# One visit less per unit, a later start for unit 4's norms, two later solves and a folded gate step in a two-layer decoder step

## The chip, the cores and the metric

The kernel runs on one core of one Trainium2 chip. The metric is device time in microseconds (us) of one execution; shown are single executions and the median of three. Its engines are TensorE (PE, with its weight loads as PEld), VectorE (DVE), ScalarE (ACT), GpSimd (POOL) and SyncE (SP, which here only issues DMAs).

## The reference, cut to what matters

One inference step of two layers for one prompt (16 meta tokens + 256) and eight samples, so 280 columns in all, width 4096, 64 heads of 64. Layer A is RWKV-7 time mixing, layer B sliding-window attention on a key/value shared by both groups. The change lies in layer A:

```python
rkvz = einsum('btpd,pde->btpe', xm[:, :, :4], w_rkvz)          # four products of 2048 x 4096
a = sigmoid(a0 + (xa @ a1) @ a2)
kk = k_h * k_k;  kk = kk / maximum(sqrt(sum(kk*kk)), 1e-12)    # norms per head
k_h = k_h * (1 + (a_h - 1) * k_a)
b_h = kk * a_h
def rwkv7_step(S, inp):                                        # scanned over the 272 prompt tokens
    r, d, k, v, kk, b = inp
    sa = einsum('bhij,bhj->bhi', S, kk)
    S = S*d - sa*b + v*k
    return S, einsum('bhij,bhj->bhi', S, r)
y = groupnorm(y) + sum(r*k*r_k) * v
hp = hp + (y * silu(z)) @ w_out
```

## The kernel before, in words

Every large product is done in split single precision: weights and inputs are cut into a high and a low part (`split`: ACT casts the high part at L195, DVE subtracts at L197), and `mm3` (L218, L219, L220) adds three matmuls, high by high, high by low, low by high.

Layer A runs from about 140 to 1245 us. `drive` writes TensorE's order by hand. Its backbone is `products()`: 64 products (r, k, v, z by groups of heads, and half of the output product) of 16 *pieces* each, a piece being six matmuls of 128x280 into one of two banks; at a product's end its banks are evacuated by ACT (L790; in the output product by DVE, L785). Between pieces other streams put in small groups of fp32 matmuls or transposes, called *visits* here: a stream says `yield n` to let n pieces pass. All other engines get their order from a scheduler, in which an instruction written after a `yield` comes later, and each runs its list strictly in that order. SP's list holds the weight loads (`raw_...`, L211, one per two pieces) and all other transfers.

The 64 heads are worked on in 16 *units* u, two to each *round* o:

- `prep(u)` loads `rT`, spreads the norms of kk over partitions (`spread`, L563, a DMA `kk<-kr`; `kr` comes by L558 from a small matrix of norms that covers four units), forms `kk` (L898), the scan `cl` (L910), `kT` (L904) and the gate `ta` (the code's `a`): ACT's affine step L905 makes a -0.5 (tanh + 1) of it, L906 multiplies by `kk`. Later it copies six tiles to `sm` on POOL (L932), forms `rk` (L945) and its split, has `ps_sm` (L935) and `ps_bo` (L954) on TensorE. `prep_e(u)` fills `KB` from `kT`, `ta` and `cl` (L972, L973).
- `scores(u)` makes five visits: two for the whole chunks' scores (L1017 ...), one for the short chunk of 16 tokens (`ps_sc4`, eight matmul records at L1031) and one each for the transposes of the keys' blocks j = 0 and 1 (`ps_bk`, ten at L1049), whose results ACT copies to `BK`.
- After the scores of an odd unit `substitute` inverts 16x16 blocks on DVE (the tile `NL`, L1075 to L1077, ends in the stream transposes TN L1081 and TR L1082, read by ACT's L1085 as `TT`), and `solve(o)` needs `TN` for its first visit (`ps_so`, L1102), then DVE's and ACT's copies for three more (L1108, L1120, L1129).
- `chain(o)` (L1191 to L1227) carries the state through the chunks, `group_norm(o)` sends y back by transposes `ps_yt` (L1275, into `vT` on DVE, L1276), and `load_x`, `decode` (the samples), `late_gates` (the output product's inputs) run beside.

`scores` and `solve` of the odd units and `chain` are one stream (`main`): a `yield` added in it moves everything behind it by as many pieces, until it next waits for another stream.

Of the kernel before, what the change touches and what calls it, by code (L numbers as in the profile page):

```python
# [25 lines left out]
L = NM + SEQ  # L26
# [83 lines left out]
class Kernel:  # L110
# [747 lines left out]
    def prep(self, u):  # L858
        nc, rp, I = self.nc, self.rp, self.I
        V, A, G = nc.vector, nc.scalar, nc.gpsimd  # L860
        tt = V.tensor_tensor
        MU, AD, SU = ALU.mult, ALU.add, ALU.subtract
        dma = nc.sync.dma_start
        p0 = 2 * u
        b, sl = p0 // 4, slice(p0 % 4, p0 % 4 + 2)
        w = lambda n, bufs=1: rp.tile([128, 2, N], F32, tag=n, bufs=bufs, name=f"{n}{u}")

        raw = rp.tile([LR, 512], F32, tag="lraw", name=f"lraw_{u}")
        dma(raw, I['lw2'][u])
        if u:  # L870
            yield 3
        hi = rp.tile([128, 544], F32R, tag="lhi", name=f"lhi_{u}")[:LR, :512]
        lo = rp.tile([128, 544], F32R, tag="llo", name=f"llo_{u}")[:LR, :512]
        self.split(hi, lo, raw)
        ws = [(hi[:, 256 * i:256 * i + 256], lo[:, 256 * i:256 * i + 256]) for i in range(2)]
        wa = [w("cl"), w("ta")]
        for i, (hi, lo) in enumerate(ws):
            for j in range(2):
                yield 3 if i or j else 4 if u else 14, self.pp_free
                ps = self.pp_bank(f"ps_l{i}{j}_{u}")  # L880
                self.mm3(ps[:, :N], hi[:, j * 128:j * 128 + 128], lo[:, j * 128:j * 128 + 128],
                         self.lt[i][0], self.lt[i][1], True, True)
# [10 lines left out]
        dma(rT, self.rd[b][:, sl])

        kk = w("kk")
        self.spread(kk, self.kr[u // 4][4 * u % 16:4 * u % 16 + 4])
        for j in range(2):
            V.scalar_tensor_tensor(kk[:, j], kT[:, j], self.pcol(P_KK, p0 + j), kk[:, j], op0=MU, op1=MU)  # L898

        for j in range(2):  # L900
            km = rp.tile([128, N], F32, tag="sq", bufs=2, name=f"km{j}_{u}")
            A.activation(km, a[:, j], AF.Identity, scale=self.par2[:, 64 + p0 + j:65 + p0 + j],
                         bias=self.par2[:, 96 + p0 + j:97 + p0 + j])
            tt(kT[:, j], kT[:, j], km, op=MU)  # L904
        A.activation(a, a, AF.Identity, scale=-0.5, bias=self.half[:, 1:2])  # L905
        tt(a, a, kk, op=MU)  # L906
        A.activation(cl, cl, AF.Identity, scale=0.5, bias=self.half[:, 0:1])

        for j in range(2):
            V.tensor_tensor_scan(cl[:, j, :L], self.reset, cl[:, j, :L], 0.0, op0=MU, op1=AD)  # L910

        Pp = self.Pp
        ch = lambda x: x[:, :, :256].rearrange("p q (c t) -> p q c t", t=64)
        pch = Pp[:, :, :260].rearrange("p q (c t) -> p q c t", t=65)
        for j in range(2):
            A.activation(pch[:, j, :, 1:65], ch(cl)[:, j], AF.Exp, scale=-CD)
        A.activation(Pp[:, :, 261:N + 5], cl[:, :, 256:N], AF.Exp, scale=-CD)
# [12 lines left out]
        sm = rp.tile([128, 2, 6, NS], F32, tag="sm", name=f"sm{u}")  # L930
        for i, x in enumerate((kk, a, kT, rT, vT, Pp[:, :, 5:])):
            G.tensor_copy(sm[:, :, i], x[:, :, L:N])  # L932
        yield 8, self.pp_free
        ps = self.pp_bank(f"ps_sm{u}")
        nc.tensor.transpose(ps[:96, :128], sm.rearrange("p a b c -> p (a b c)"), self.ident)  # L935
        sr = rp.tile([96, 2, 64], F32, tag="sr", name=f"sr{u}")
        A.copy(sr, ps[:96, :128].rearrange("p (h j) -> p h j", h=2))  # L937
        g, h0 = p0 // 8, (2 * p0) % 16
        for j in range(2):
            dma(self.vecd[g][:, :, h0 + 2 * j:h0 + 2 * j + 2].rearrange("v b h j -> (v b) (h j)"),  # L940
                sr[48 * j:48 * j + 48].rearrange("p h j -> p (h j)"))

        def rk_of(j):
            rk = rp.tile([128, L], F32, tag="sq", bufs=2, name=f"rk{j}_{u}")
            V.scalar_tensor_tensor(rk, rT[:, j, :L], self.pcol(P_RK, p0 + j), kT[:, j, :L], op0=MU, op1=MU)  # L945
            self.split(two[0][:, j], two[1][:, j], rk)
        two = [rp.tile([128, 2, L], F32R, tag=n, name=f"rk{n}{u}") for n in ("lhi", "llo")]
        for j in range(2):
            rk_of(j)
        for j in range(2):  # L950
            yield 5 - j if u > 1 else 3, self.pp_free
            ps = self.pp_bank(f"ps_bo{j}_{u}")
            for i in range(2):
                nc.tensor.matmul(ps[:, :L], self.ones, two[i][:, j], start=i == 0, stop=i == 1)  # L954
            tt(vT[:, j, :L], ps[:, :L], vT[:, j, :L], op=MU)
            A.activation(vT[:, j, :L], vT[:, j, :L], AF.Identity, bias=self.pcol(P_GB, p0 + j))
        self.U[u] = dict(PC=self.PC, bonus=vT, kT=kT, rT=rT, kk=kk, a=a, cl=cl)

    def prep_e(self, u):
# [12 lines left out]
        tt(KB[:, :, 0:4, 0:64], ch(a), ch(cl), op=MU)  # L972
        tt(KB[:, :, 4, 0:16], a[:, :, 256:272], cl[:, :, 256:272], op=MU)  # L973
        A.copy(KB[64:128, :, :, 128:192], KB[64:128, :, :, 0:64])

        E = rp.tile([128, 5, 2, L], F32, tag="E", bufs=3, name=f"E_{u}")
# [7 lines left out]
    def scores(self, u):  # L984
        nc, rp = self.nc, self.rp

        odd = u % 2
        gap = iter((8, 3, 4, 3, 3) if odd else (8, 6, 6, 5, 4))
        turn = iter((0, odd, 0, odd, 0))
        def banks(nm):  # L990
            if next(turn):
                two = self.two_banks(f"ps_{nm[0]}{nm[1]}")
# [14 lines left out]
        for c0 in (0, 2):  # L1007
# [11 lines left out]
            for q in range(2):  # L1019
                pv, kr = ps[q], H(1 - q)  # L1020
                out = lambda i, r: E[r, i, :, 64 * c0:64 * c0 + 128].rearrange("p a (c t) -> p a c t", c=2)
                for r, a, t0 in ((64 * q, self.F, 0), (64 * q + 32, self.ND, 32)):
                    A.copy(inst(a, slice(r ^ 64 * odd, (r ^ 64 * odd) + 32), cs), pv[r:r + 32, :, :, t0:64])
                tt(out(q, kr), pv[kr, :, :, 0:64], bc(self.cst(C_MASK, 64, kr), 64, 2, 2, 64), op=MU)
                tt(out(3 + q, slice(0, 128)), pv[:, :, :, 64:128], bc(self.cst(C_MASK + 64, 64), 128, 2, 2, 64), op=MU)
        yield next(gap)
        ps = [b[:, :64].rearrange("p (a h t) -> p a h t", a=2, h=2) for b in banks(("sc", f"4_{u}"))]
        with self.pe_order():
            for j in range(2):
                for q in (1, 0):  # L1030
# [12 lines left out]
        for j in range(2):
            yield next(gap)
            ps = [b[:, :320].rearrange("p (c t) -> p c t", c=5) for b in banks(("bk", f"{j}_{u}"))]
            with self.pe_order():
                for c in range(5):
                    for q in (1, 0):
                        nc.tensor.transpose(ps[q][:, c], KB[H(q), j, c, 64 * q:64 * q + 128], self.ident[H(q), H(q)])  # L1049
            for q in range(2):  # L1050
                A.copy(BK[:, j, :, H(q)], ps[q])
# [37 lines left out]
    def solve(self, o):  # L1089
# [4 lines left out]
        ev = lambda n, *s: rp.tile([128, 512], F32, tag="ev", bufs=2, name=f"{n}{o}")[:, :s[0] * s[1]].rearrange(  # L1094
            "p (i t) -> p i t", t=s[1])

        yield 24 if o < 5 else 27
        ps = self.bank(self.pe, f"ps_so{o}")
        Q = [slice(32 * q, 32 * q + 32) for q in range(4)]
        for i in range(16):  # L1100
# [872 lines left out]
```

## Time and profile before

| | us |
|---|---|
| three runs | 2115.4, 2117.19, 2122.31 (median 2117.19) |
| profiled execution, whole | 2118.32 |
| its span | 2116.5 |
| TensorE busy in the span | 2064.9 (98%) |
| VectorE busy | 1697.8 (80%) |
| ScalarE busy | 1263.8 (60%) |
| GpSimd busy | 122.5 (6%) |
| mean granted TensorE clock | 0.99 of full speed |

The 1.8 us between the span and the whole execution lie outside the profile. TensorE's idle time, 51.6 us, is spread over the program, and an engine that is busy in the records may still be slow: the column PEclk of the profile's stretches gives the clock that it was granted. In the rows below a line is "start, duration, engine, line, operation, output<-input", and a bracket at the end holds how long the engine had stood idle before it and what released it.

### The profile page before, as it was taken

Reading aid. Unit: us, or ns where it says so; the run is one execution under the profiler, and the core shown is the slowest. Engines: PE = TensorE matmul, PEld = TensorE weight load, DVE = VectorE, ACT = ScalarE, POOL = GpSimd, SP = SyncE. Lnnn points to the kernel's source line nnn. Section 1 sums busy time; section 2 is a strip of 40 time slices with the busy share of each in tenths; the row PEclk is TensorE's granted clock in tenths of the full one; section 3 lists DMA queues with packets and bytes.
Section 4 is the critical chain, followed back from the end, with each engine's and each line's share of the span. In section 5 each row is a group of like instructions: output and inputs, shape, how many; then the busy total and the mean of one; then the engine's idle time right before and its main releaser. Section 6 shows DMA issues by size and latency. Waiting matters only on the chain.

```text
span 2116.5 us, 55871 instructions
## 1 busy us (share of the span) xinstructions
PE 2064.9 (98%) x21420; PEld 1965.8 (93%) x21420; DVE 1697.8 (80%) x4112; ACT 1263.8 (60%) x2790; POOL 122.5 (6%) x188
## 2 busy tenths in 40 slices
PE   9999999899999999999999999999999999999997
PEld 7999899889899989899999999999999999999997
DVE  8867777687678878888888788997888888878885
ACT  3457766576766757767676445565565655544443
POOL 0011100001010010100100001100000000000000
PEclk9999999999999999999999999999999999999999
DMA  7898667658756876777657687757455444567774
GB/s 258 314 312 250 189 213 241 188 181 290 216 180 205 260 229 198 211 217 222 203 152 246 207 257 243 247 172 227 132 167 156 146 155 130 181 210 247 232 219 132
DMA packets 276356, 446.28 MB, mean 211 GB/s; under 512 B 54056, under 2 KB 97768, under 8 KB 275696
## 3 DMA queue, kind: packets, MB, share of 16 engines
q1 hardware_dynamic: 275656, 441.66, 66.6%
q8 instruction: 168, 2.75, 0.5%
q10 hardware_dynamic: 432, 1.05, 0.1%
q14 instruction: 100, 0.82, 0.1%
HBM read 381.69 MB, written 65.03 MB: 211 GB/s over the span
## 4 chain that ended last, share of the span: by engine, by line
PE 87%; DVE 5%; ACT 3%; DMA 3%; issue 2%; SPq 0%; POOL 0%; DVEq 0%; POOLq 0%; ACTq 0%
PE ps_z L218 6%; PE ps_z L219 6%; PE ps_z L220 6%; PE ps_k L218 3%; PE ps_ob L218 3%; PE ps_ob L220 3%; PE ps_v L218 3%; PE ps_ob L219 3%; PE ps_r L218 3%; PE ps_q L218 3%; PE ps_q L220 3%; PE ps_q L219 3%; PE ps_k L219 3%; PE ps_k L220 3%; PE ps_v L220 3%; PE ps_v L219 3%
## 5 line engine op out<-in xcount | busy, mean ns | idle before, releaser
L218 PE MATMUL ps_z<-mhlm,whi_z 128*128 128x280 f32 x512 | 158.6, 310 | 2.8 <-ACT sr L937 2.0
L219 PE MATMUL ps_z<-mhlm,whi_z 128*128 128x280 f32 x512 | 150.6, 294 | 0.0
L220 PE MATMUL ps_z<-mhlm,wlo_z 128*128 128x280 f32 x512 | 150.3, 294 | 0.0
L218 PE MATMUL ps_q<-bmh,whi_qb 128*128 128x264 f32 x512 | 150.0, 293 | 0.1
L218 PE MATMUL ps_z<-bmh,whi_zb 128*128 128x264 f32 x512 | 147.4, 288 | 0.0
L220 PE MATMUL ps_q<-bmh,wlo_qb 128*128 128x264 f32 x512 | 145.6, 284 | 0.6 <-DVE wlo_qb L197 0.6
L219 PE MATMUL ps_q<-bml,whi_qb 128*128 128x264 f32 x512 | 145.6, 284 | 0.0
L219 PE MATMUL ps_z<-bml,whi_zb 128*128 128x264 f32 x512 | 145.5, 284 | 0.0
L220 PE MATMUL ps_z<-bmh,wlo_zb 128*128 128x264 f32 x512 | 145.4, 284 | 0.0
L218 PE MATMUL ps_ob<-ghi,whi_ob 128*128 128x264 f32 x512 | 145.3, 285 | 0.0
L220 PE MATMUL ps_ob<-ghi,wlo_ob 128*128 128x264 f32 x512 | 144.6, 284 | 0.0
L219 PE MATMUL ps_ob<-glo,whi_ob 128*128 128x264 f32 x512 | 144.6, 283 | 0.0
L195 ACT CAST whi_ob<-raw_ob 128x512 fp32r<-128x512 f32 x128 | 79.1, 620 | 96.9 <-PE ps_ob L219 77.8
L195 ACT CAST whi_oa<-raw_oa 128x512 fp32r<-128x512 f32 x128 | 79.2, 620 | 88.0 <-PE ps_oa L219 30.6
L197 DVE TENSOR_TENSOR wlo_r<-raw_r,whi_r 128x512 fp32r<-128x512 f32 x128 | 87.8, 691 | 42.6 <-ACT whi_r L195 41.3
L218 PE MATMUL ps_v<-mhlm,whi_v 128*128 128x280 f32 x384 | 119.8, 312 | 0.4 <-ACT st L790 0.4
L218 PE MATMUL ps_k<-mhlm,whi_k 128*128 128x280 f32 x384 | 119.1, 310 | 1.0 <-ACT st L790 1.0
L195 ACT CAST whi_v<-raw_v 128x512 fp32r<-128x512 f32 x128 | 79.0, 619 | 65.8 <-PE ps_v L219 37.7
L197 DVE TENSOR_TENSOR wlo_v<-raw_v,whi_v 128x512 fp32r<-128x512 f32 x128 | 87.3, 687 | 36.9 <-ACT whi_v L195 35.6
L195 ACT CAST whi_zb<-raw_zb 128x512 fp32r<-128x512 f32 x128 | 78.2, 619 | 62.9 <-PE ps_z L219 38.5
L220 PE MATMUL ps_k<-mhlm,wlo_k 128*128 128x280 f32 x384 | 112.4, 293 | 2.1 <-issue 2.1
L219 PE MATMUL ps_v<-mhlm,whi_v 128*128 128x280 f32 x384 | 112.7, 293 | 0.0
(478 smaller groups left out, 7604.1 us busy)
## 6 DMA issues: line engine op xcount, KB each, us to landing
raw_k<-a_w_rkvz SPq DMA_DIRECT2D x128, 256.0 KB
raw_v<-a_w_rkvz SPq DMA_DIRECT2D x128, 256.0 KB
raw_r<-a_w_rkvz SPq DMA_DIRECT2D x128, 256.0 KB
raw_z<-a_w_rkvz SPq DMA_DIRECT2D x128, 256.0 KB
raw_oa<-a_w_out SPq DMA_DIRECT2D x128, 256.0 KB
raw_qb<-b_w_qz SPq DMA_DIRECT2D x128, 256.0 KB
raw_zb<-b_w_qz SPq DMA_DIRECT2D x128, 256.0 KB
raw_ob<-b_w_o SPq DMA_DIRECT2D x128, 256.0 KB
```

The source lines that it names most:

```text
L195: self.nc.scalar.copy(hi, src)
L197: return self.nc.vector.tensor_tensor(lo, src, hi.bitcast(F32), op=ALU.subtract)
L218: mm(ps, wh, xh, start=start, stop=False)
L219: mm(ps, wh, xl, start=False, stop=False)
L220: return mm(ps, wl, xh, start=False, stop=stop)
```

## The change

Five edits, all in layer A:

1. The ten transposes of the block j = 0 stand in the visit of the short chunk's scores, in the same two banks; the visit of their own falls away, and the gaps become 8, 3, 4, 3 (odd units) and 8, 6, 6, 6.
2. `prep(4)` lets ten pieces pass between the load of `rT` and the norms.
3. `solve`'s first visit: 24 and 27 pieces were counted from a visit that now stands earlier, so the same place reads 27 and 30; solve 0 reads 32, five pieces later than before, and solve 5 reads 34, four later.
4. The gate's affine step leaves ACT: DVE forms (a + 1) * kk, and the factor -0.5 goes into the two products that fill `KB` (which become three DVE instructions) and into POOL's copy to `sm`.
5. `rk` and its split are written ahead of the wait for the sample visit, right behind the scan's copies.

```diff
+        if u == 4:
+            yield 10
         kk = w("kk")
         self.spread(kk, self.kr[u // 4][4 * u % 16:4 * u % 16 + 4])
...
-        A.activation(a, a, AF.Identity, scale=-0.5, bias=self.half[:, 1:2])
-        tt(a, a, kk, op=MU)
+        V.scalar_tensor_tensor(a, a, 1.0, kk, op0=AD, op1=MU)
...
+        two = [rp.tile([128, 2, L], F32R, tag=n, name=f"rk{n}{u}") for n in ("lhi", "llo")]
+        for j in range(2):
+            rk_of(j)
         if u >= 4:
             yield 0, self.after(0, ('g', u // 2 - 2))
...
-            G.tensor_copy(sm[:, :, i], x[:, :, L:N])
+            if i == 1:
+                G.tensor_scalar(sm[:, :, i], x[:, :, L:N], -0.5, None, op0=MU)
+            else:
+                G.tensor_copy(sm[:, :, i], x[:, :, L:N])
         yield 8, self.pp_free
...
-        for j in range(2):
-            rk_of(j)
...
-        tt(KB[:, :, 0:4, 0:64], ch(a), ch(cl), op=MU)
-        tt(KB[:, :, 4, 0:16], a[:, :, 256:272], cl[:, :, 256:272], op=MU)
+        for j in range(2):
+            stt(KB[:, j, 0:4, 0:64], ch(a)[:, j], -0.5, ch(cl)[:, j], op0=MU, op1=MU)
+        stt(KB[:, :, 4, 0:16], a[:, :, 256:272], -0.5, cl[:, :, 256:272], op0=MU, op1=MU)
...
-        gap = iter((8, 3, 4, 3, 3) if odd else (8, 6, 6, 5, 4))
+        gap = iter((8, 3, 4, 3) if odd else (8, 6, 6, 6))
...
+        both = banks(("sc", f"4_{u}"))
...
+            turned(both, 0)
...
+        kept(both, 0)
+        yield next(gap)
+        both = banks(("bk", f"1_{u}"))
+        with self.pe_order():
+            turned(both, 1)
+        kept(both, 1)
...
-        yield 24 if o < 5 else 27
+        yield {0: 32, 5: 34}.get(o, 27 if o < 5 else 30)
```

TensorE's list has 373 visits in layer A where it had 385. Three places show what moved.

The first is TensorE at unit 0's short chunk. Before, the scores alone stand between two pieces of a product (`ps_sc` are the two banks, `KB` and `E` their inputs, `ps_r` the product):

```order
L220 MATMUL ps_r_0_2359<-mhld_5_1516,wlo_r_10_2450 128x280
L1031 MATMUL ps_sc_0_2531<-E_2218,KB 128x32
L1031 MATMUL ps_sc_0_2530<-E_2218,KB 128x32
L1031 MATMUL ps_sc_0_2531<-E_2218,KB 128x32
L1031 MATMUL ps_sc_0_2530<-E_2218,KB 128x32
L218 MATMUL ps_r_1_2360<-mhld_5_1516,whi_r_10_2449 128x280
```

Now the transposes (L1037, of `KB` with an identity from `consts`; the first two of ten) follow in the same visit:

```order
L220 MATMUL ps_r_0_2359<-mhld_5_1516,wlo_r_10_2450 128x280
L1049 MATMUL ps_sc_0_2540<-E_2218,KB 128x32
L1049 MATMUL ps_sc_0_2539<-E_2218,KB 128x32
L1049 MATMUL ps_sc_0_2540<-E_2218,KB 128x32
L1049 MATMUL ps_sc_0_2539<-E_2218,KB 128x32
L1037 MATMUL ps_sc_0_2540<-consts,KB 128x64
L1037 MATMUL ps_sc_0_2539<-consts,KB 128x64
```

One switch from the product to small work and back is gone.

The second is VectorE at unit 4's `kk`, in round 1's substitution. Before, `kk` stands in the middle of the substitution's last steps, and TN, TR and the `vT` of round 0 (which frees the bank of `ps_yt`) are behind it:

```order
L898 SCALAR_TENSOR_TENSOR kk_5449<-kT_5445,par,kk_5449 128x280
L1075 TENSOR_TENSOR stmp_14_5118<-NL_5077 128x28
L898 SCALAR_TENSOR_TENSOR kk_5449<-kT_5445,par,kk_5449 128x280
L910 SCALAR_TENSOR_TENSOR cl_4871<-reset,cl_4871 128x272 x2
L904 TENSOR_TENSOR kT_5445<-kT_5445,km_4_5454 128x280
L1077 TENSOR_TENSOR NL_5077<-NL_5077,stmp_14_5118 128x2x14
L197 TENSOR_TENSOR wlo_v_14_5425<-raw_v_14_5422,whi_v_14_5424 128x512
L904 TENSOR_TENSOR kT_5445<-kT_5445,km_4_5457 128x280
L906 TENSOR_TENSOR ta_4872<-ta_4872,kk_5449 128x560
L1081 STREAM_TRANSPOSE TN_5123<-NL_5077 128x512
L1082 STREAM_TRANSPOSE TR_5124<-NL_5077 128x512
L1276 SCALAR_TENSOR_TENSOR vT_2043<-ps_yt_0_5399,par,vT_2043 128x272
```

Now the substitution ends and `vT` is done first:

```order
L1093 TENSOR_TENSOR NL_5129<-NL_5129,stmp_14_5170 128x2x14
L1097 STREAM_TRANSPOSE TN_5175<-NL_5129 128x512
L1098 STREAM_TRANSPOSE TR_5176<-NL_5129 128x512
L197 TENSOR_TENSOR wlo_v_4_5475<-raw_v_4_5472,whi_v_4_5474 128x512
L1292 SCALAR_TENSOR_TENSOR vT_2052<-ps_yt_0_5431,par,vT_2052 128x272 x2
L197 TENSOR_TENSOR wlo_v_6_5481<-raw_v_6_5478,whi_v_6_5480 128x512
L900 SCALAR_TENSOR_TENSOR kk_5614<-kT_5415,par,kk_5614 128x280 x2
L911 SCALAR_TENSOR_TENSOR cl_4904<-reset,cl_4904 128x272 x2
```

`kk` stood right behind the weight split `wlo_v` 12 of one product and stands behind 6 of the next: five splits further, of which one comes per two pieces. On SP the DMAs `kk<-kr` stand one weight load further back.

The third is TensorE at solve 0's first visit (`ps_so`), which stood in the middle of the piece pair of weights 2:

```order
L219 MATMUL ps_r_0_3391<-mhld_1_1292,whi_r_2_3366 128x280
L220 MATMUL ps_r_0_3391<-mhld_1_1292,wlo_r_2_3367 128x280
L1102 MATMUL ps_so_3430<-TN_3007,Noff 32x16 x64
L218 MATMUL ps_r_1_3392<-mhld_1_1292,whi_r_2_3366 128x280
L219 MATMUL ps_r_1_3392<-mhld_1_1292,whi_r_2_3366 128x280
```

and now stands behind the piece pair of weights 6, with the small product `ps_l` (unit 3's) in the same place:

```order
L219 MATMUL ps_r_1_3382<-mhld_3_1486,whi_r_6_3391 128x280
L220 MATMUL ps_r_1_3382<-mhld_3_1486,wlo_r_6_3392 128x280
L1118 MATMUL ps_so_3473<-TN_3012,Noff 32x16 x64
L218 MATMUL ps_l_3_3540<-lt5h,lhi_3324 128x280
L219 MATMUL ps_l_3_3540<-lt5l,lhi_3324 128x280
```

It moved from piece 211 to piece 216 of the 1120, and with it all of `main` up to piece 403, where both orders agree again; they agree (but for the merged visits) to piece 778. Solve 5 moved from 778 to 782, and `main` stays four pieces later to its last visit, at piece 1097 before and 1101 now. The output product's second half starts at piece 1120 in both.

More of the change, by code (lines that the diff above doesn't have):

```diff
@@ L923, in prep, with rk_of @@
         A.copy(PC[:, :, 4:5], Pp[:, :, 276:277])
+        def rk_of(j):
+            rk = rp.tile([128, L], F32, tag="sq", bufs=2, name=f"rk{j}_{u}")
+            V.scalar_tensor_tensor(rk, rT[:, j, :L], self.pcol(P_RK, p0 + j), kT[:, j, :L], op0=MU, op1=MU)
+            self.split(two[0][:, j], two[1][:, j], rk)
+        two = [rp.tile([128, 2, L], F32R, tag=n, name=f"rk{n}{u}") for n in ("lhi", "llo")]
+        for j in range(2):
+            rk_of(j)
         if u >= 4:
@@ L941, in prep @@
                 sr[48 * j:48 * j + 48].rearrange("p h j -> p (h j)"))
[L943 to L947, printed above, removed]
-        for j in range(2):
-            rk_of(j)
         for j in range(2):
@@ L971, in prep_e @@
         tt(KB[:, :, 4, 64:80], kT[:, :, 256:272], cl[:, :, 256:272], op=MU)
-        tt(KB[:, :, 0:4, 0:64], ch(a), ch(cl), op=MU)
-        tt(KB[:, :, 4, 0:16], a[:, :, 256:272], cl[:, :, 256:272], op=MU)
+        stt = V.scalar_tensor_tensor
+        for j in range(2):
+            stt(KB[:, j, 0:4, 0:64], ch(a)[:, j], -0.5, ch(cl)[:, j], op0=MU, op1=MU)
+        stt(KB[:, :, 4, 0:16], a[:, :, 256:272], -0.5, cl[:, :, 256:272], op0=MU, op1=MU)
         A.copy(KB[64:128, :, :, 128:192], KB[64:128, :, :, 0:64])
@@ L987, in scores @@
         odd = u % 2
-        gap = iter((8, 3, 4, 3, 3) if odd else (8, 6, 6, 5, 4))
-        turn = iter((0, odd, 0, odd, 0))
+        gap = iter((8, 3, 4, 3) if odd else (8, 6, 6, 6))
+        turn = iter((0, odd, 0, odd))
         def banks(nm):
@@ L1025, in scores, with turned, kept @@
                 tt(out(3 + q, slice(0, 128)), pv[:, :, :, 64:128], bc(self.cst(C_MASK + 64, 64), 128, 2, 2, 64), op=MU)
+        blocks = lambda two, j: [b[:, 64 - 64 * j:384 - 64 * j].rearrange("p (c t) -> p c t", c=5) for b in two]
+        def turned(two, j):
+            for c in range(5):
+                for q in (1, 0):
+                    nc.tensor.transpose(blocks(two, j)[q][:, c], KB[H(q), j, c, 64 * q:64 * q + 128], self.ident[H(q), H(q)])
+        def kept(two, j):
+            for q in range(2):
+                A.copy(BK[:, j, :, H(q)], blocks(two, j)[q])
         yield next(gap)
-        ps = [b[:, :64].rearrange("p (a h t) -> p a h t", a=2, h=2) for b in banks(("sc", f"4_{u}"))]
+        both = banks(("sc", f"4_{u}"))
+        ps = [b[:, :64].rearrange("p (a h t) -> p a h t", a=2, h=2) for b in both]
         with self.pe_order():
@@ L1041, in scores @@
             self.substitute(u // 2)
[L1043 to L1051, printed above, removed]
+        kept(both, 0)
[4 more added lines that the diff above has]
+        kept(both, 1)
     def substitute(self, o):
```

## The prediction

> **What bounds the kernel now.** I read the page's busy table and chain first, then the waits of TensorE stretch by stretch, then the timeline at each place that the change touches, and last the granted clock there.
>
> ```profile
> PE 2064.9 (98%) x21420; PEld 1965.8 (93%) x21420; DVE 1697.8 (80%) x4112; ACT 1263.8 (60%) x2790; POOL 122.5 (6%) x188
> PE 87%; DVE 5%; ACT 3%; DMA 3%; issue 2%; SPq 0%; POOL 0%; DVEq 0%; POOLq 0%; ACTq 0%
> ```
>
> TensorE is the bound and the chain runs through it. So a change pays if TensorE has fewer things to do, stands less, or runs at a higher clock; work added on the other engines costs only where TensorE then waits. Where it stands is seen from the stretches (start:end, length, busy of PE, PEld, DVE, ACT, POOL, then clock, DMA share, GB/s):
>
> ```profile
> 250.00:461.00 211.00, 198.02 (x2754) 183.89 (x2753) 154.57 (x352) 135.28 (x306) 11.53 (x22) 0.97 0.65 207
> 461.00:905.00 444.00, 433.31 (x5409) 405.40 (x5408) 349.74 (x802) 308.49 (x693) 41.12 (x60) 0.99 0.72 223
> 905.00:1246.00 341.00, 333.82 (x4499) 314.87 (x4498) 290.13 (x662) 217.81 (x473) 17.36 (x31) 0.98 0.66 206
> ```
>
> Idle time is length less PE busy: 13.0, 10.7 and 7.2 us, in the second stretch in waits of at most 2.0:
>
> ```profile
> PE ps_bo L954 <- ACT vk L854: 2.0, 1, 2.0
> ```
>
> The first and third stretch are those that the edits shift by four or five pieces; in the second the order only loses visits. The three waits at the places that are moved, and one at a solve that is not (665.87):
>
> ```profile
> 255.14 1.05 DVE L1081 STREAM_TRANSPOSE TN<-NL 128x512 f32<-128x512 f32 x1
> 256.24 1.27 PE L1102 MATMUL ps_so<-TN,Noff 32*32 32x16 f32 x128 [3.50 <-DVE TN L1081]
> 375.65 0.51 DVE L898 SCALAR_TENSOR_TENSOR kk<-kT,par,kk 128x280 f32<-128x280 f32 x1 [4.24 <-DMA kk<-kr]
> 381.45 0.46 DVE L1276 SCALAR_TENSOR_TENSOR vT<-ps_yt,par,vT 128x272 f32<-128x272 f32 x1
> 381.96 0.90 PE L1275 MATMUL ps_yt<-consts,Y 128*128 128x128 f32 x3 [6.92 <-DVE vT L1276]
> 665.87 1.20 PE L1129 MATMUL ps_so<-TT,ET 32*32 32x32 f32 x64 [1.23 <-ACT ET L1124]
> 913.43 1.90 PE L1102 MATMUL ps_so<-TN,Noff 32*32 32x16 f32 x128 [2.56 <-DVE TN L1081]
> ```
>
> Solve 0 and solve 5 reach TensorE 3.50 and 2.56 us before TN is there. At 375 the reader is to see a blocked queue: VectorE stood 4.24 us for the norms of unit 4 with the `vT` that frees TensorE's bank behind them, and TensorE stood 6.92.
>
> A wait has an aftermath. Rows of one us each, the column after the five engines being the granted clock:
>
> ```profile
> 258.00:259.00 1.00, 1.00 (x6) 1.00 (x5) 0.00 (x0) 1.00 (x2) 0.00 (x0) 0.50 0.00 0
> 384.00:385.00 1.00, 1.00 (x7) 1.00 (x6) 0.00 (x0) 1.00 (x2) 0.00 (x0) 0.50 0.80 279
> 668.00:669.00 1.00, 1.00 (x7) 1.00 (x6) 0.49 (x1) 0.00 (x0) 0.00 (x0) 0.50 1.01 303
> 785.00:786.00 1.00, 1.00 (x6) 1.00 (x6) 0.00 (x0) 0.00 (x0) 0.00 (x0) 0.50 0.88 306
> 918.00:919.00 1.00, 1.00 (x6) 1.00 (x6) 0.00 (x0) 0.51 (x1) 0.00 (x0) 0.50 0.84 307
> 1050.00:1051.00 1.00, 1.00 (x6) 1.00 (x6) 1.00 (x2) 0.00 (x0) 0.00 (x0) 0.50 0.37 135
> ```
>
> TensorE is busy in each, yet at half clock, and starts six or seven matmuls in a us. Six such spells lie between 140 and 1246 us; three follow the waits above.
>
> ```profile
> 257.44 0.60 PE L218 MATMUL ps_r<-mhld,whi_r 128*128 128x280 f32 x1
> 261.02 0.29 PE L218 MATMUL ps_r<-mhld,whi_r 128*128 128x280 f32 x1
> 261.79 0.29 PE L218 MATMUL ps_r<-mhld,whi_r 128*128 128x280 f32 x1
> 382.52 0.58 PE L218 MATMUL ps_v<-mhlm,whi_v 128*128 128x280 f32 x1
> 387.27 0.38 PE L218 MATMUL ps_v<-mhlm,whi_v 128*128 128x280 f32 x1
> 915.26 0.60 PE L218 MATMUL ps_z<-mhlm,whi_z 128*128 128x280 f32 x1
> 919.77 0.29 PE L218 MATMUL ps_z<-mhlm,whi_z 128*128 128x280 f32 x1
> ```
>
> From 261.02 to 261.79 six matmuls start, 0.13 apiece: a piece lasts 0.77 us. From 257.44 to 261.02 fifteen start in 3.58 us, at full clock 2.0: 1.5 lost (rounded down for the switch). From 382.52 to 387.27 eighteen and a visit take 4.75, at full clock some 2.8: 2.0 lost. From 915.26 to 919.77 eighteen and one transpose take 4.51 for 2.5, 2.0 lost, and the solve before them 1.83 where solve 0 took 1.20: 2.6 in all. Together 6.1 us, which the idle column does not show.
>
> The Trainium skill ("TensorE: Matmul & The Clock Gate", Part 1, What's actually happening) says that the clock halves after an idle window of about 3.4 us and recovers after as long a busy one. The length of the spells agrees (257.4 to 261), the trigger only partly: by it the waits of 2.56 and 1.23 would have none behind them; the rows show them (918, 668), so I price spells by the rows. By the rule alone solve 5's 2.6 would not hang on its wait, and the sum below would come out at -9.9.
>
> **The change part by part.** *The merged visit.* What a visit costs beside its own matmuls:
>
> ```profile
> 203.13 0.29 PE L220 MATMUL ps_r<-mhld,wlo_r 128*128 128x280 f32 x1
> 203.35 0.52 PE L1049 MATMUL ps_bk<-consts,KB 64*128 64x64 f32 x10
> 203.80 0.40 PE L218 MATMUL ps_r<-mhld,whi_r 128*128 128x280 f32 x1
> 204.04 0.29 PE L219 MATMUL ps_r<-mhld,whi_r 128*128 128x280 f32 x1
> 306.74 0.41 PE L1208 MATMUL ps_ch<-X,E 64*64 64x64 f32 x16
> 307.08 0.52 PE L1049 MATMUL ps_bk<-consts,KB 64*128 64x64 f32 x10
> ```
>
> The step into a visit takes 0.22 (203.13 to 203.35) and the second step behind it 0.24 (203.80 to 204.04), where steps between product matmuls take 0.13: 0.20 too much. The step from the last small matmul to the product, some 0.20 by the single records, is exchanged for a join of scores and transposes, some 0.16 where L1049 follows L1208 at 307.08: 0.24 net. TensorE's list loses 14 round trips, since two of the 16 transposes had shared a visit with other work: 14 x 0.24 = 3.4 us, all on the path. Ends: 0 (the join costs as much as the trip) and 16 x 0.24 = 3.9.
>
> *Unit 4's norms.* Ten pieces are 7.7 us. VectorE came to them at 371.41 and would come at 379.1 by the same clock; they landed at 375.65, and one weight load more ahead of them on SP (one per two pieces) makes about 377.2. The margin is 2 us, and TN, TR and `vT` no longer stand behind them. So 6.9 and the spell's 2.0 go: 8.9. What is late next is the third `ps_yt`, whose `vT` does stand behind `kk`. Ends: 8.9, and 2.0 if the norms are as late again with that `vT` behind them.
>
> *The solves.* Five pieces are 3.9 us against 3.50, four are 3.1 against 2.56: both waits are covered, with 0.4 and 0.5 to spare, and with their spells give 3.5 + 1.5 and 2.6 + 2.6, 10.2. Behind solve 0's first visit ACT's copies and the evacuation of the product at piece 224 now meet (below). Ends: 10.2, and 4.1 if waits of 1 us remain that keep the spells (as the wait at 665.87 has the spell at 668).
>
> *The gate, POOL's copy and `rk`.*
>
> ```profile
> L905 ACT ACTIVATE ta<-ta,half x16: 757/762/774, 164.8 to 1081.6; 128x560 f32<-128x560 f32 x16
> L972 DVE TENSOR_TENSOR KB<-ta,cl x16: 678/685/689, 173.4 to 1100.9; 128x512 f32<-128x512 f32 x16
> 870.16 0.64 SPq L893 DMA_DIRECT2D rT<-rd  x1
> 878.31 0.20 POOL L932 COPY sm<-rT 128x16 f32<-128x16 f32 x1 [37.71 <-DMA rT<-rd]
> 888.49 0.45 DVE L904 TENSOR_TENSOR kT<-kT,km 128x280 f32<-128x280 f32 x1
> 907.46 0.91 DVE L945 SCALAR_TENSOR_TENSOR rk<-rT,par,kT 128x272 f32<-128x272 f32 x2
> 909.70 0.43 DVE L197 TENSOR_TENSOR rkllo<-rk,rklhi 128x272 fp32r<-128x272 f32 x1
> ```
>
> ACT loses 16 x 0.76 = 12.2 us; VectorE does one more instruction per unit and cuts 0.69 into two halves, estimated +0.2 each, 3 us in all; POOL stays as it is, busy 6%. The cover is TensorE's stream: VectorE is 20% idle, ACT 40%. `rk` needs `rT` and `kT`; the slowest `rT` of all (870.16 issued, in use at 878.31) lands ten us ahead of its `kT`, so no queue blocks on it from unit 1 on, and unit 0 waits as before. I take 0, ends -1 and +3.
>
> *What comes back.* Two stretches, 211 + 341 = 552 us, get new meetings of the streams. The unshifted stretch between them has 10.7 us idle and two spells (668, 785) of about 1.5 in 444: 13.7, 3.1 per 100 us, which is what an order without a remarkable fault loses here. For 552 us that is 17.0; uncured there stay 20.2 - 13.0 = 7.2 idle and the spell of 1050, 8.7. So 8.3 would come back. By the rate of all three (30.9 idle, 6.1 + 4.5 of spells in 996 us, 4.2 per 100) it would be 14. Named places: solve 1's ACT run `TT` (four of 0.87, in the row below), which now falls on the product boundary at piece 320, up to 3; the meeting at 224, up to 2; the output product's banks behind late group-norm work at 1097 to 1105, up to 3; each with a spell at worst.
>
> ```profile
> 381.56 3.13 ACT L1085 ACTIVATE TT<-TR,consts 128x320 f32<-128x320 f32 x4 [1.26 <-DVE TR L1082]
> ```
>
> I take 10, nearer the rate that has no cured place in it.
>
> Sum: -3.4 - 8.9 - 10.2 + 0 + 10 = -12.5. The profiled execution took 2118.3 (1.1 above the median, 1.8 above its span), so 2105.8; for the median 2117.2 - 12.5 = 2104.7, say **2105**.
>
> **The rivals.** *All of it comes back:* the moved work finds other waits as large (2 to 3 us each with a spell, at the three places), 19 us return and only the merged visits are left: 2114. For it speaks that the orders of `main` and the preparations were placed against each other, and five pieces break that everywhere from 230 to 403; against it the second stretch, where no wait exceeds 2.0 us. *Nothing comes back:* 2117.2 - 22.5 = 2095; against it, every stretch has its ten us. *The norms do not get in time:* the spread goes later with the ten pieces, VectorE stands again, and only the rest is gained: 2105 + 7 = 2112. SP's order speaks against it. *Slower:* VectorE gets per unit a solid block, `kT`, the gate, `rk` and its splits, 1.8 us more of it (`rk` 0.91 for both, two splits of 0.43) than before, with weight splits behind it. If these came late for TensorE in each unit, 1.8 a time, with a spell of 1.5, 16 units cost 53; it turns the forecast into a slowdown of 0.3% from (12.5 + 6.4) / 3.3 = six units on, and at eight the time is 2105 + 26 = 2131. Against it: no wait for a `wlo` in layer A is among those of note, and the block leaves a place a few us later. *The merged visit slows the clock:* were small work no work to the clock's gate, the 26 small records in a row that end at 307.5 should be followed by a spell; there is none in the trace. It would cost up to 16 x 1.5 = 24, 2129. The Trainium skill (the same page, Part 4, PE-mode transpose) says that transposes do not count as busy in the same way; the trace here shows no sign of it.
>
> **How the numbers follow.** Forecast 0.62, all comes back 0.17, nothing comes back 0.06, norms late 0.10, slower by the block 0.04, by the clock 0.01. Measurement can tell about 0.3%, 6.4 us, from no change: faster means under 2110.8. From the forecast (0.60 of its 0.62), the clean case and a third of the late norms: 0.69; slower over 2123.5: 0.05; between: 0.26. The range goes from just above the clean case, 2096, over the forecast to the case in which all comes back with 1 us of the gate's upper end: 2115. The forecast's own is 2099 to 2111.
>
> **What the next profile would show.** Fewer PE visits and no L1049 of its own for j = 0; at solve 0 and 5 brackets under 1 us and a clock of 1.00 behind them; at the first `ps_yt` no wait over 2 and VectorE's `kk` without its 4.24; in the second stretch idle time of about 10 as now. Waits of 2 us and more with half clock behind them near pieces 224, 320 or 1100 would be what came back. Wrong is the forecast if idle plus spells in the shifted stretches do not fall by 10.

## The result and the profile after

The changed kernel took 2106.95 us (median of 7 runs) against 2117.19 before: ratio 0.9954, 95% interval 0.9936 to 0.9971. A second comparison, below, gave 0.9962 (0.9948 to 0.9976). So the change is worth 8 to 10 us, 0.4%; 2105 was forecast.

The profiled execution took 2104.34 us, the fastest of the seven; its span is 2102.5, 14.0 under the span before, so its rows show more gain than the median does. The stretches that were shown of before, in the kernel after (clock, DMA share, GB/s at the end):

```profile
PE 2053.3 (98%) x21420; PEld 1956.4 (93%) x21420; DVE 1696.2 (81%) x4128; ACT 1252.7 (60%) x2774; POOL 122.4 (6%) x188
250.00:461.00 211.00, 205.79 (x2899) 191.32 (x2898) 161.48 (x369) 139.04 (x321) 10.25 (x22) 0.99 0.70 217
461.00:905.00 444.00, 432.87 (x5608) 406.42 (x5607) 354.64 (x830) 307.44 (x687) 42.12 (x62) 0.99 0.74 229
905.00:1246.00 341.00, 328.44 (x4245) 310.14 (x4244) 285.11 (x642) 211.23 (x459) 16.29 (x29) 0.99 0.65 207
```

TensorE's idle time is 5.2, 11.1 and 12.6 us where it was 13.0, 10.7 and 7.2: the first stretch gained 7.8, the third lost 5.4. (The stretches are cut by time; the kernel after is ahead by then, so they do not hold quite the same work.) Over the whole span idle time fell by only 2.4 us, from 51.6 to 49.2. The other 11.6 us are busy time, for the same 21420 matmuls: fewer round trips, and above all fewer us at half clock. By the clock records of the two traces, half clock cost 12.6 us of matmul time between 130 and 1300 us before and costs 4.8 now (half of TensorE's busy time in it), and 1.7 at 1391 went too. In rows of one us, 16 are below a clock of 0.96 between 130 and 1260 us where 35 were; those that fall into a wait cost nothing.

Part of that is luck. The wait of 1.23 us for `ET` that had a spell of half clock behind it at 668 is still there, as long as before, and now has none:

```profile
649.09 1.10 PE L1145 MATMUL ps_so<-TT,ET 32*32 32x32 f32 x58 [1.23 <-ACT ET L1140]
651.00:652.00 1.00, 1.00 (x11) 1.00 (x10) 0.00 (x0) 0.02 (x1) 0.00 (x0) 1.00 1.00 225
```

The same holds for a wait of 1.77 us behind layer A (at 1389.57 before, at 1376.74 now). The places of the prediction:

```profile
254.65 1.27 PE L1118 MATMUL ps_so<-TN,Noff 32*32 32x16 f32 x128 [0.58 <-DVE TN L1097]
372.49 0.55 PE L1291 MATMUL ps_yt<-consts,Y 128*128 128x128 f32 x3 [1.57 <-DVE vT L1292]
375.42 0.60 PE L218 MATMUL ps_v<-mhlm,whi_v 128*128 128x280 f32 x1 [1.61 <-ACT st L790]
375.72 0.93 DVE L900 SCALAR_TENSOR_TENSOR kk<-kT,par,kk 128x280 f32<-128x280 f32 x2
895.79 1.27 PE L1118 MATMUL ps_so<-TN,Noff 32*32 32x16 f32 x128
```

3.50, 6.92 and 2.56 became 0.58, 1.57 and none, 10.8 us less, and VectorE's `kk` waits for no DMA. The merged visit:

```profile
195.93 0.29 PE L220 MATMUL ps_r<-mhld,wlo_r 128*128 128x280 f32 x1
196.16 0.63 PE L1049 MATMUL ps_sc<-E,KB 64*128 64x32 f32 x8
196.62 0.51 PE L1037 MATMUL ps_sc<-consts,KB 64*128 64x64 f32 x10
197.06 0.40 PE L218 MATMUL ps_r<-mhld,whi_r 128*128 128x280 f32 x1
197.29 0.29 PE L219 MATMUL ps_r<-mhld,whi_r 128*128 128x280 f32 x1
```

From the L220 ahead to the second product matmul behind it is 1.36 us. The two visits took 0.91 (203.13 to 204.04) and, for the scores, 1.02 by the rows of before:

```profile
198.11 0.29 PE L220 MATMUL ps_r<-mhld,wlo_r 128*128 128x280 f32 x1
199.13 0.29 PE L219 MATMUL ps_r<-mhld,whi_r 128*128 128x280 f32 x1
```

The two visits held two product steps of 0.13 more, so the trip saved is 1.93 - 1.36 - 0.26 = 0.31 us, 14 times 4.3; by the 12 visits that TensorE's list lost (385 to 373) it is 3.7.

What came back came back chiefly in two kinds of wait. The first is at the end of layer A, where `main` is now four pieces late. A transpose of the samples' output `dy` and the last state transposes wait for VectorE; 1248.17 is the last visit of `main`. Below them is the stretch with these waits, and then the same stretch of the kernel before:

```profile
1233.16 0.30 PE L1353 MATMUL ps_dy<-consts,dy 128*64 128x128 f32 x1 [1.85 <-DVE dy L1350]
1240.46 0.55 PE L1291 MATMUL ps_yt<-consts,Y 128*128 128x128 f32 x3 [2.03 <-DVE vT L1292]
1244.29 0.55 PE L1291 MATMUL ps_yt<-consts,Y 128*128 128x128 f32 x3 [0.97 <-DVE vT L1292]
1248.17 0.55 PE L1291 MATMUL ps_yt<-consts,Y 128*128 128x128 f32 x3 [1.03 <-DVE vT L1292]
1225.00:1265.00 40.00, 33.85 (x257) 32.72 (x257) 29.21 (x66) 16.65 (x26) 0.00 (x0) 1.00 0.80 264
```

```profile
1225.00:1265.00 40.00, 39.95 (x369) 38.79 (x368) 37.31 (x92) 21.72 (x38) 0.20 (x1) 1.00 0.82 258
```

That is 6.15 us idle where there was next to none. Over the whole layer TensorE's waits at the state transposes add to 8.7 us in seven places, where they were 8.0, nearly all in the one of 6.92.

The second kind the prediction did not name. "Issue" is idle time for which the profile shows no releaser; TensorE's in the solves' second visit, before (first row) and after:

```profile
PE ps_so L1108 <- issue: 1.7, 1, 1.7
```

```profile
PE ps_so L1124 <- issue: 8.4, 4, 3.9
764.51 0.25 PE L1124 MATMUL ps_so<-TR,ET 32*16 32x16 f32 x7 [3.94 <-issue]
1029.88 0.22 PE L1124 MATMUL ps_so<-TR,ET 32*16 32x16 f32 x2 [2.88 <-issue]
761.00:762.00 1.00, 0.00 (x0) 0.00 (x0) 0.00 (x0) 0.00 (x0) 0.00 (x0) 0.50 0.96 376
766.00:767.00 1.00, 1.00 (x6) 1.00 (x6) 0.85 (x2) 0.00 (x0) 0.00 (x0) 0.50 0.08 31
```

121 of the 128 records had run, then TensorE stood for 3.94 us in the middle of a visit, with all inputs there; from 761 to 762 no engine worked and the DMAs did. Half clock began with the wait and lasted three us beyond it. With the waits at product matmuls (before 2.1 at L220; after 0.9, 0.6, 0.5 and 0.4) issue was 3.8 us and is 10.8.

### The profile page after: what moved, and what is told of

It reads as the page before. It is cut to its first block, busy times and chain, and to the rows that moved or that the text cites. A ratio compares the mean times of both kernels' runs of the same rounds, so it can differ in the third digit from the quotient of the medians.

```text
span 2102.5 us, 55860 instructions
## 1 busy us (share of the span) xinstructions
PE 2053.3 (98%) x21420; PEld 1956.4 (93%) x21420; DVE 1696.2 (81%) x4128; ACT 1252.7 (60%) x2774; POOL 122.4 (6%) x188
## 5 line engine op out<-in xcount | busy, mean ns | idle before, releaser
L220 PE MATMUL ps_z<-mhlm,wlo_z 128*128 128x280 f32 x512 | 149.6, 292 | 0.0
L220 PE MATMUL ps_q<-bmh,wlo_qb 128*128 128x264 f32 x512 | 145.5, 284 | 0.2 <-DVE wlo_qb L197 0.2
L220 PE MATMUL ps_z<-bmh,wlo_zb 128*128 128x264 f32 x512 | 145.4, 284 | 0.0
L220 PE MATMUL ps_ob<-ghi,wlo_ob 128*128 128x264 f32 x512 | 144.6, 284 | 0.0
L218 PE MATMUL ps_v<-mhlm,whi_v 128*128 128x280 f32 x384 | 119.4, 311 | 2.1 <-ACT st L790 1.6
L220 PE MATMUL ps_k<-mhlm,wlo_k 128*128 128x280 f32 x384 | 112.3, 293 | 0.9 <-issue 0.9
L197 DVE TENSOR_TENSOR wlo_k<-raw_k,whi_k 128x512 fp32r<-128x512 f32 x112 | 76.6, 688 | 45.2 <-ACT whi_k L195 44.9
```

What stands on the lines that cost most here:

```text
L197: return self.nc.vector.tensor_tensor(lo, src, hi.bitcast(F32), op=ALU.subtract)
L218: mm(ps, wh, xh, start=start, stop=False)
L220: return mm(ps, wl, xh, start=False, stop=stop)
```

## The experiments

Each was timed over five rounds against the kernel before. Ratio with its 95% interval, and the sum of the issue waits that the profile lists between 130 and 1300 us:

| kernel | what it is | ratio | issue, us |
|---|---|---|---|
| p1_merge | edit 1 alone | 0.9984 (0.9969 to 0.9998) | 6.0 |
| p2_wait | edit 2 alone | 0.9997 (0.9984 to 1.001) | 5.8 |
| p3_solves | edit 3 alone | 0.9977 (0.9964 to 0.9991) | 8.6 |
| p4_gate | edits 4 and 5 alone | 0.9993 (0.9978 to 1.0009) | 6.9 |
| r_nowait | all but edit 2 | 0.9971 (0.9957 to 0.9985) | 8.8 |
| r_nosolves | all but edit 3's delays | 0.9977 (0.9963 to 0.9990) | 9.5 |
| full | all, once more | 0.9962 (0.9948 to 0.9976) | 8.1 |
| q16 | all, 64 instructions more at the start | 0.9914 (0.9896 to 0.9932) | 3.8 |
| mid16 | all, 64 instructions more in solve 4's last visit | 0.9926 (0.9911 to 0.9940) | 7.9 |
| w24 | all, 96 instructions more at the opening's end | 0.9935 (0.9917 to 0.9953) | 4.8 |
| w32 | all, 128 instructions more there | 0.9937 (0.9922 to 0.9951) | 6.9 |
| q48 | all, 192 instructions more at the start | 0.9970 (0.9957 to 0.9982) | 10.5 |

### The edits one at a time

The merged visits, with the solves where they were:

```diff
-        gap = iter((8, 3, 4, 3, 3) if odd else (8, 6, 6, 5, 4))
+        gap = iter((8, 3, 4, 3) if odd else (8, 6, 6, 6))
+            turned(both, 0)
-        yield 24 if o < 5 else 27
+        yield 27 if o < 5 else 30
```

> The merged visits alone (edit 1, with the solves at their old places: 27 and 30 pieces). My theory: 14 round trips of 0.24 us less, -3.4, so 2113.8 against a median of 2117.2, with the waits of 3.5 (solve 0), 6.9 (unit 4's norms) and 2.6 (solve 5) still there, each with its spell of half clock behind it. The rival that a join costs as much as a trip: no change, 2117. The rival that small work in longer runs slows the clock: spells behind the merged visits and up to +24.

-3.4 us measured, as expected (the interval reaches from -0.4 to -6.6). No merged visit has a spell behind it.

Unit 4's ten pieces:

```diff
+        if u == 4:
+            yield 10
         kk = w("kk")
```

> Unit 4's ten pieces alone (edit 2). My theory: the wait of 6.9 at the first state transposes of round 0 goes with its spell of 2.0, -8.9, so 2108.3, with VectorE's wait of 4.24 for the norms gone too. The rival that the norms go later with the ten pieces: VectorE still waits for them, TensorE stands 4 us or more, and the time stays within 2 of 2117.

Nothing measured, and yet not for the rival's reason: the wait went. In the one profile of this kernel what the stretch gained there it lost 45 us later. The first two rows are this kernel, the last is the kernel before:

```profile
380.40 0.55 PE L1277 MATMUL ps_yt<-consts,Y 128*128 128x128 f32 x3 [0.84 <-DVE vT L1278]
425.00:461.00 36.00, 32.68 (x352) 29.58 (x351) 29.93 (x81) 23.83 (x62) 1.41 (x5) 0.86 0.42 129
```

```profile
425.00:461.00 36.00, 34.52 (x452) 31.59 (x442) 30.28 (x81) 26.07 (x69) 1.88 (x6) 1.00 0.55 173
```

Between 425 and 461 the idle time rose from 1.5 to 3.3 us and the clock fell from 1.00 to 0.86, which is 4.6 of the 32.7 busy us: 6.4 of the 8.9 expected came back in one place. In rows: waits at the chain and at a product's end (1.72 on L790), spells behind both. The two stretches do not hold quite the same work (352 and 452 matmuls), so that the gain was given back there is read from one profile and not shown. This profile also has a spell at 172 that the kernel before had not, ahead of the edit's place, so not the edit's doing, and solve 4's issue wait was 3.17.

The later solves:

```diff
-        yield 24 if o < 5 else 27
+        yield {0: 29, 5: 31}.get(o, 24 if o < 5 else 27)
```

> The two later solves alone (edit 3, 29 pieces for solve 0 and 31 for solve 5, counted from the old visit). My theory: 3.5 + 1.5 and 2.6 + 2.6 go, -10.2, less what comes back in the two shifted stretches, 2 to 6 of waits at product ends, so 2109 to 2113. The rival that all comes back elsewhere: 2117.

-4.9 us, inside my bracket (2117.2 x 0.9977 = 2112.3). It showed that the edits overlap: with edit 2 left out, the state transposes now wait

```profile
380.52 0.90 PE L1275 MATMUL ps_yt<-consts,Y 128*128 128x128 f32 x3 [2.35 <-DVE vT L1276]
```

2.35 us instead of 6.92. VectorE still waits for the norms, in the middle of a substitution that also comes later; but the `vT` now stands ahead of the substitution's last steps, where it had stood behind them and the transposes TN and TR:

```profile
373.27 0.93 DVE L898 SCALAR_TENSOR_TENSOR kk<-kT,par,kk 128x280 f32<-128x280 f32 x2 [2.68 <-DMA kk<-kr]
379.97 0.50 DVE L1276 SCALAR_TENSOR_TENSOR vT<-ps_yt,par,vT 128x272 f32<-128x272 f32 x1
383.21 1.10 DVE L1081 STREAM_TRANSPOSE TN<-NL 128x512 f32<-128x512 f32 x1
```

The gate's fold and the earlier `rk`:

```diff
-        A.activation(a, a, AF.Identity, scale=-0.5, bias=self.half[:, 1:2])
-        tt(a, a, kk, op=MU)
+        V.scalar_tensor_tensor(a, a, 1.0, kk, op0=AD, op1=MU)
```

> The gate's fold and the earlier product for the bonus alone (edits 4 and 5). My theory: 12 us less on ScalarE and 3 more on VectorE, both hidden, within 1 us of 2117, the three waits as before. The rival that VectorE's block of 1.8 us more per unit makes weight splits late: +1.8 for each unit where it meets them, up to 2146.

No change that can be told (-1.5, from -4.7 to +1.9). ScalarE is 7.8 us less busy and VectorE 1.4 more (1256.0 and 1699.2), and both are hidden. Of the waits it stood beside two stayed and were longer (4.33 at solve 0, 8.13 at the state transposes); that at solve 5 was 1.03.

### All but one

The changed kernel without the lines of edit 2, and with `yield 27 if o < 5 else 30` in `solve`:

> The changed kernel without edit 2 (unit 4's norms where they were). The prediction's step: the wait at round 0's first state transposes comes back with 6.9 and its spell, +8.9, ratio to the kernel before 0.9996. The theory after the single edits: the later solve 0 alone already shortened that wait to 2.35, so only 2 to 4.5 come back, ratio 0.996 to 0.997.

> The changed kernel with both solves at their old places (27 and 30 pieces). The prediction's step: 3.5 + 1.5 and 2.6 + 2.6 come back, and what came back elsewhere through the shift goes, +2 to +10, ratio 0.996 to 1.000. The theory after the single edits (the two later solves alone gave 0.9977): +4.9, ratio 0.9977. Rival (the solves' places don't matter once the norms wait): 0.9954 as with them.

0.9971 and 0.9977 against 0.9954 (0.9962 the second time): edit 2 is worth about 2 to 4 us in company, edit 3 about 3 to 5, as the second theory had it and a quarter to a half of the prediction's steps. Each ratio has an interval of some 3 us to either side, so neither is well clear of nothing, and the issue sums of these kernels (8.1 to 10.8) differ by 2.7 us. The rows of r_nowait, then r_nosolves:

```profile
371.57 0.93 DVE L898 SCALAR_TENSOR_TENSOR kk<-kT,par,kk 128x280 f32<-128x280 f32 x2 [3.14 <-DMA kk<-kr]
379.84 0.90 PE L1289 MATMUL ps_yt<-consts,Y 128*128 128x128 f32 x3 [3.37 <-DVE vT L1290]
```

```profile
254.18 1.76 PE L1118 MATMUL ps_so<-TN,Noff 32*32 32x16 f32 x128 [4.04 <-DVE TN L1097]
903.90 1.90 PE L1118 MATMUL ps_so<-TN,Noff 32*32 32x16 f32 x127 [3.08 <-DVE TN L1097]
```

VectorE waits for the norms again, but TensorE only 3.37; and without the delays both solves wait as before. The waits are cured by the edits that were meant for them; what the wait was worth was the smaller number.

For edit 3 the profiles show a price. The wait of 1.85 us for `dy` stands in all nine kernels with the later solves and in none of the five with the solves at their old places; of the two solves only solve 5's delay lasts to the end. From 1225 to 1300 us TensorE waits 2.3 to 6.15 us in the nine and 0 to 0.7 in the five (0.7 in r_nosolves).

### The wait on issue

One queue of the profile's page, q8, moves "instruction" packets in a number that fits TensorE:

```profile
q8 instruction: 168, 2.75, 0.5%
```

168 packets of 16.4 KB for 2 x 21420 records of matmuls and weight loads: one packet per 255 records. A solve's visit is 128 of each, one packet's worth in 1.25 us, where the products use that much in some 16 us. In the kernel after no packet of that queue ran between 738.8 and 755.7 us, and three did from there to 767, around the wait (rows of the DMA view for the two stretches: the queues that moved anything):

```profile
q1 hardware_dynamic: 2227, 4.23, 79.4%
q14 instruction: 2, 0.02, 0.2%
```

```profile
q1 hardware_dynamic: 1475, 3.39, 82.2%
q8 instruction: 3, 0.05, 1.6%
```

In that wait, from 760.57 to 764.51, one packet ran (761.9 to 763.1; none from 756.8 to 761.9, none from 763.1 to 764.6):

```profile
q8 instruction: 1, 0.02, 5.1%
```

So the theory: TensorE ran out of code. The Trainium skill ("Runtime: NRT & Kernel Launch", Instruction fetch mechanics) has each engine fetch blocks of 256 instructions ahead on a queue of its own and calls the crossing mostly hidden; the block's size agrees with the 255 here, the hiding does not hold in a dense visit.

The packet records of the traces bear the theory out. This packet began at 762.01, 1.44 us after TensorE had stopped, landed at 763.00, and TensorE went on 1.51 us later. All 76 issue waits that the 14 profiles list between 130 and 1300 us end 1.16 to 1.72 us after the queue's latest packet landed; a moment picked at random does so in one of twenty cases. In the nine waits over 3 us the packet began 0.8 to 1.4 us after TensorE had stopped. If it is the code's place, moving all code by part of a block must move the waits:

```diff
             filling(5)
+            for _ in range(16):   # 48 in q48
+                nc.tensor.matmul(junk[:16, :16], ones[:32, :16], fill[:32, :16], start=True, stop=True)
```

> The same with 16 small matmuls (64 instructions, a quarter of a block). The block theory: the solves begin at 0.00, 0.61, 0.66, 0.24, 0.85, 0.20, 0.84, 0.41, so the waits on issue leave solves 4 and 6 and appear at solves 1 and 2 (3 us each with spells), ratio about 0.995 as without them. Rival: solves 4 and 6 wait as before, solves 1 and 2 do not.

> The changed kernel with 48 small matmuls into an unused bank added in the first microseconds (192 more instructions on TensorE, under 1 us of work), nothing else. New theory: TensorE's code comes in blocks of 256 instructions (168 transfers of 16 KB on one queue), and the waits 'on issue' at the solves' second visit come where a solve begins at 0.55 to 0.66 of a block (solves 4 and 6 of the changed kernel: 3.9 and 2.9). Three quarters of a block more move the eight solves to 0.50, 0.11, 0.16, 0.74, 0.35, 0.70, 0.34, 0.91, none in the bad range: the two waits go with their spells, 6.8 + 3 less, ratio to the kernel before about 0.991. Rival (the waits belong to those visits, whatever the code's place): solves 4 and 6 wait as before, ratio 0.995.

q16 is the fastest kernel of all: its waits on issue fell from 10.8 to 3.8 us, solve 4's from 3.94 to 0.71 and solve 6's to nothing:

```profile
762.50 0.91 PE L1126 MATMUL ps_so<-TR,ET 32*16 32x16 f32 x89
764.12 0.50 PE L1126 MATMUL ps_so<-TR,ET 32*16 32x16 f32 x39 [0.71 <-issue]
1027.23 1.24 PE L1126 MATMUL ps_so<-TR,ET 32*16 32x16 f32 x128
```

The wait's place in the visit moved one for one with the code. It stands behind 121 of the 128 records in the kernel after and behind 89 in q16, which has 32 matmul records more ahead of it; behind 25 in q48 (96 more):

```profile
767.73 0.38 PE L1126 MATMUL ps_so<-TR,ET 32*16 32x16 f32 x25
769.74 1.03 PE L1126 MATMUL ps_so<-TR,ET 32*16 32x16 f32 x103 [1.63 <-issue]
```

w24 and w32 (48 and 64 more) have it behind 73 and 57. But the rule of the expectations for how long the waits are failed twice. (Its places are the parts of a block of 256 instructions at which a solve begins, counted in the code.) Solves 1 and 2, at the bad places 0.61 and 0.66, waited 0.76 and 0.84 instead of 3, and q48, forecast best, kept 10.5 us. Part of q48's time is another cost: in the opening the 96 records held up the order that TensorE shares with VectorE, and TensorE stood 4.1 us for the first input of the products (0.7 in q16):

```profile
PE ps_k L253 <- DVE mst L393: 4.1, 1, 4.1
```

That leaves the start of the program as an explanation for q16 too, so the next kernel has the same 64 instructions behind solve 4's last dense visit:

```diff
-        for i in range(16):
+        for i in (*range(8 if o == 4 else 0), *range(16)):
             for q in range(2):
                 r = Q[2 * q + 1]
                 nc.tensor.matmul(ps[Q[2 * q], i], ET[r, i], TT[r, i, 32:64], start=True, stop=True)
```

> The changed kernel with 16 small matmuls repeated in the last visit of solve 4 (64 instructions on TensorE, the quarter block of the earlier test, but placed after solve 4's dense visits; 0.3 us of work). The code's place theory: solve 4 waits on issue as in the changed kernel (3 to 4 us, its code is where it was), the wait at solve 6 (2.9) goes as it did when the 64 instructions stood at the program's start, ratio about 0.9935. Rival (what helped there was the start of the program, not the code's place): solve 6 waits as before, ratio 0.995.

> The changed kernel once more, beside the next three on one chip: ratio to the kernel before 0.9954 as in the first comparison, the waits on issue near 11 us in layer A with 3 us or more at solve 4's second visit, which all kernels with that code place have shown.

The rows of mid16 at solves 4 and 6, then of full:

```profile
768.52 0.25 PE L1124 MATMUL ps_so<-TR,ET 32*16 32x16 f32 x7 [3.39 <-issue]
1030.64 1.25 PE L1124 MATMUL ps_so<-TR,ET 32*16 32x16 f32 x128
```

```profile
770.69 0.25 PE L1124 MATMUL ps_so<-TR,ET 32*16 32x16 f32 x7 [3.11 <-issue]
1039.72 0.22 PE L1124 MATMUL ps_so<-TR,ET 32*16 32x16 f32 x2 [1.73 <-issue]
```

Ahead of the inserted code the wait stands, with the same seven records left; behind it the wait is gone. That is the code's place, and the start of the program is out. The ratio, 0.9926 against 0.9962 on the same chip, is more than the 1.7 us of that wait explain, and the issue sums of the two profiles are alike (7.9 and 8.1; full's profiled execution, 2115.6 us, was its slowest). The granted clock of all runs explains about half: its mean is 0.9940 in mid16's six and 0.9920 in full's seven, and 0.0020 of 2110 us is 4.2 of the 7.6 us between their means. The rest is open.

Two more places, with the small matmuls behind `filling(7)`, where they cost less:

> The changed kernel with 24 small matmuls (96 instructions) late in the opening phase, behind the filling matmuls. By place of code the solves begin at 0.12, 0.73, 0.79, 0.37, 0.98, 0.32, 0.96, 0.54 of a block. The waits seen so far at a given place were 3 to 5 us at 0.35 to 0.65 and under 1 at 0.85 to 1.0, so solves 4 and 6 wait under 1 us, issue in all 2 to 6, ratio 0.990 to 0.993. Rival (no rule by place): anything from 0.990 to 0.997.

> The same with 32 small matmuls (128 instructions, half a block): places 0.25, 0.86, 0.91, 0.49, 0.10, 0.45, 0.09, 0.66. By place solves 4 and 6 wait little, solves 3 and 5 (0.49, 0.45) and 7 (0.66) are in the bad range: issue in all 4 to 9, ratio 0.992 to 0.996. Rival as above.

Both came within their brackets for the issue sum (4.8 of 2 to 6, 6.9 of 4 to 9) and, but for w24's ratio of 0.9935 at 0.990 to 0.993, for the time. Solves 4 and 6 were as expected in w24 (0.82 and none). In w32 solve 4 waited 1.41, and of the three solves named as bad only the last waited (1.95). So where a wait stands follows from the code, but how long it is does not follow from the place alone. Solve 4 waited 3.94, 3.11 and 3.39 behind 121 records, 1.69 to 3.65 behind 115 to 120 (the kernel before, and all single and left-out edits but p4_gate), 0.71 behind 89, 0.82 behind 73, 1.41 behind 57, 1.63 behind 25; in p4_gate it waited nothing, and a product matmul ahead of it 2.85. Solve 4's traffic is dense (DMA share 0.96 from 757.5 to 764 in q16), solves 1 and 2 of q16 have 0.64 and 0.63. A packet that is late under traffic would fit them, but solve 6 of the kernel after waited 2.88 with a share of 0.65, so why a packet begins late stays open.

## Why the prediction was right, point by point

It gave 2105, -12.5 us; measured were -9.7 and -8.0. The waits went as it said, but their worth was taken too high, and what came back was the right size in part from other places. Its steps:

- The merged visit: 3.4 forecast, 3.4 measured alone, 3.7 to 4.3 by the rows (0.31 a trip for 0.24; the join is cheaper than taken, and the list lost 12 visits, not 14).
- Unit 4's norms: 8.9 forecast, nothing alone, 2 to 4 in company. The mechanism was right (the DMA wait, the blocked queue and the 6.92 went), the size was off: the end "2.0" was nearer. The term took the whole wait as the edit's, though edit 3 shortened the same wait to between 2.35 and 3.37, and alone it seems to have been given back at 425 to 461, where the next units' work then met.
- The solves: 10.2 forecast, about 5 alone and about 3 to 5 in company; both waits went, 6.1 us of brackets became 0.6. At the end of layer A the later solve 5 cost 2.3 to 6.15 us of it again.
- The gate, POOL's copy and `rk`: 0 forecast, -1.5 (+1.9 to -4.7) measured.
- What comes back: 10 forecast. The parts of 22.5 less the 9.7 measured leave 12.8. Of the named places solve 1's `TT` at the product boundary is there (1.61 at 375.42), and so is the late group-norm work near piece 1100, with 6.15 where "up to 3" was named, though in waits for VectorE and hardly (0.28) for the output product's banks; at solve 0's second visit there is no wait for ScalarE. In none of them were 7.0 us more of issue, from the code's place, with the spells at solves 4 and 6.
- The clock's spells: 6.1 us of gain counted for them that the idle column does not show; by the clock records 7.8 were gained in layer A. But the three spells that the edits aimed at were worth 7.4 by these records, three others went that no edit aimed at (5.1), and three new ones came (4.8). The second profile of the same kernel, full, has 13.4 us of half clock in layer A, more than the kernel before.
- Its own sign of being wrong was met: by its prices idle plus spells in the shifted stretches fell from 20.2 + 7.6 to 17.8 + 3.0, by 7.0 and not by 10. The profile gained outside them too (1.6 us of idle time between 130 and 250, the spells at 667, 783 and 1391), so that the time came so near the forecast is in part luck.

The single edits add to -0.49% (-0.16, -0.03, -0.23, -0.07) and the whole gave -0.46%: small terms near the end of what 12 runs can tell. The rate of the unshifted stretch, as a price for what comes back, gave about the right size, in part by luck.

## What to carry to other kernels

Where one engine is 98% busy, price a wait on it with what follows it, the us at half clock, and price two edits that ease one wait once. Work that is moved meets something else: a stretch's usual loss per 100 us is a better guess of that than nothing. Work that is made later is felt where its stream ends: look there first. And before a change of under 1% is called good or bad, look at the waits on issue and at the half clock: a shift of the code by 64 instructions was worth as much here as the whole change (0.9914 against 0.9954), with no change in what is computed. Other insertions gave 0.9926 to 0.9970, the last no better than none.

## What the runs showed of the hardware that I had not expected

- TensorE waits for its own code in dense visits of small matmuls, up to 3.94 us. The place moves one for one with inserted matmuls (121, 89, 73, 57, 25 records into solve 4's visit), and all 76 such waits end 1.16 to 1.72 us after a packet of its instruction queue landed. Why some packets begin only after TensorE has stopped is open.
- Half clock can follow waits much shorter than a spell: 1.23 us at 665.87 in the kernel before was enough, and the same wait in the kernel after was not. By the clock records all spells of a profile begin on one raster of 3.413 us: those of the kernel before at 257.48, 376.95, 667.08, 783.13, 912.84 and 1049.37 lie 35, 85, 34, 38 and 40 steps apart. Over the 14 profiles (130 to 1300 us), of the steps of that raster at full clock, all 37 in which TensorE was idle for 1.9 us or more were followed by half clock, 27 of 114 with 1.0 to 1.9 us, and 1 of 4544 with less. So a wait of 2 us that falls across the border of two steps can go free. A spell lasts one step or more (3.4 to 10.2 us) and costs at most 1.7 us of matmul time per step.
